# Two-layer hybrid mixer step on one core: value products with 128 weight columns, three more projections by seven products, PSUM copies on ScalarE

## The chip, the cores and the metric

One core of one Trainium2 chip runs the whole program in one launch. The metric is the device time of that launch in microseconds, lower is better; before the change it is 1943.42 us (median of three runs, 1942.09 to 1944.15).

## The reference

Two layers run over 512 prompt positions and 32 sample positions (544 columns in all), model width 1024, in float32. A layer multiplies the residual stream `h` by one wide input projection, whose columns feed four token mixers of four heads of 64 each, and gates:

```
pr = split_projection(h @ w_in)
A: stick-breaking:  z = q k^T / 8; w = exp(log_sigmoid(z) + sum of later log_sigmoid(-z)); y = w v
B: retention:       q, k = rotary(q), rotary(k) / 8; S' = g^c S + (k * decay)^T v
                    o = ((q k^T) * decay) v + (q S) * g^(n+1); y = head_norm(o) * silu(gate)
C: forgetting:      softmax(q k^T / 8 + cq - ck) v
D: sparse:          softmax over the 128 (sample: 72) keys that an indexer picks, one shared k and v head
merged = sum_i sigmoid(gate_i) * (y_i @ w_branch_i)
h = LN(ALPHA h + merged @ w_out); h = LN(ALPHA h + SwiGLU(h))
```

The prompt starts with an empty past, the sample has a cache of 256 positions and a retention state. The outputs are `h` and the new caches and states.

## The kernel before

**Layout.** Activations are kept transposed, features on the partitions and the 544 columns in two halves of `HB` = 272. Each operand of a large product is split into two reduced-precision parts, high (by ScalarE) and low (by VectorE, the remainder), and a product is three TensorE instructions: high x high, high x low, low x high.

**Two kinds of projection.** `dense` (L733) multiplies 128 output columns: weights `raw` are split into `whi` and `wlo`, and for each half eight blocks of depth take three matmuls each, 48 in all, 96 for a pair of column blocks. `strassen` (L786) makes a pair of column blocks for both halves at once with seven products instead of eight (84 matmuls): it needs sums of weight blocks (`ws`, `wt` by accumulating DMAs of GpSimd's queue, `wsum` by VectorE), splits seven operands `wop`, and adds up the results `st`, `su`, `sv` on VectorE. Its right side are differences of `h` blocks, `T`. `proj2` (L921) uses it for retention's values, `merge` (L1653) for all gates, `ffn` for most of the feed-forward part. Retention's queries, keys and gate use `proj` and `dense`.

**Mixers.** `fox` (L1297) and `dsa` (L1373) go through four row blocks and four heads: scores into PSUM, maximum, exponential, division by the sum, four or fewer transposes, a copy `pT` of those out of PSUM, and then the product with the values. That product takes the head's 64 value columns as weights and writes half of the partitions of a bank, `o[r, ...]`, for s = 0 the lower and for s = 1 the upper half. `stick` (L1425) does all heads' products of a row block together; `pv_sample` (L1360) does them for the sample. The values are plain float32, for which one matmul of the program is two passes in the trace.

**Retention** (L1532): the projections of queries and keys are rotated by `rotary` (L1499): four DMAs swap partition groups into `xs`, GpSimd multiplies by the cosine, VectorE by the sine, VectorE adds. Four chunks of 128 columns follow, each with scores, state and `head_norm_T`; the gate's sigmoid is made from exp (ScalarE), add (GpSimd) and reciprocal (VectorE) in `silu` (L1544).

**Copies.** `ev` (L683) copies out of PSUM, on VectorE and ScalarE in turn.

**Order.** Every operation is recorded first (so every instruction of the profile has the line L661, and groups are told apart by tile names). `schedule` (L555) then simulates a list scheduler with its own costs and priorities and sets each engine's order; `fillers` (L637) puts small idle matmuls where that simulation leaves TensorE without work; `places` and `fit` (L180, L206) choose buffer addresses. `build` repeats this up to five times, each from the draft before, and keeps the one whose simulated end is earliest. Each engine's queue runs strictly in the order set.

```
def ev(...):            # L683
    if eng is None:
        self.flip ^= 1
        eng = "v" if self.flip else "s"
...
nc.tensor.matmul(o[r, p * 128:(p + 1) * 128], v[:, j, h * 64:(h + 1) * 64], pT[:, j, :],   # fox
                 start=j == 0, stop=j == i)
```

## Time and profile before

| | us |
|---|---|
| runs before: median (lowest to highest) | 1943.42 (1942.09 to 1944.15) |
| the profiled execution | 1947.43 |
| its span, first to last instruction | 1945.7 |
| TensorE busy in it | 1881.4 (97%) |
| VectorE busy | 1601.7 (82%) |
| ScalarE busy | 1043.9 (54%) |
| GpSimd busy | 499.8 (26%) |

The mean granted TensorE clock over the span is 0.991 of full speed. TensorE's rows are matmuls (PE) and weight loads (PEld), which overlap; a matmul's recorded length is longer than the distance to the next one, so what one costs is read from the distance of starts. The first layer ends at about 970 us, the second begins there.

### The profile page before, as it was taken

What the parts mean: (1) busy time and instruction counts of PE and PEld (TensorE: products, weight loads), DVE (VectorE), ACT (ScalarE), POOL (GpSimd) and SP (SyncE); (2) the same over time, 40 slices, a digit from 0 to 9 for tenths busy, and PEclk for the clock granted to TensorE, in tenths of its full rate; (3) what the DMA queues carried; (4) which work ended last, traced back from release to release, by engine and by line L of the source; (5) the groups of instructions that cost most, each with busy time, mean ns of one, the idle gap of its engine ahead of it and who ended that gap; (6) DMA issues with size and microseconds to landing.
All of it is one profiled execution on the core that took longest, in us unless ns stands there. A gap on an engine that the chain in (4) does not pass through costs nothing.

```text
span 1945.7 us, 39164 instructions
## 1 busy us (share of the span) xinstructions
PE 1881.4 (97%) x14619; PEld 1801.8 (93%) x14619; DVE 1601.7 (82%) x3549; ACT 1043.9 (54%) x2160; POOL 499.8 (26%) x500
## 2 busy tenths in 40 slices
PE   9999999999999999999999999899999999999997
PEld 8997789999998999999989978889999999999996
DVE  5988769787879889888778886697879799899875
ACT  4565535555546656556455563355556375565552
POOL 0343031234341111321413331302433301114101
PEclk9999999999999999999999999999999999999999
DMA  8322244666632687777313132347675237777741
GB/s 226 85 72 69 52 101 91 150 153 144 155 105 77 143 199 168 175 169 182 103 32 99 56 96 52 79 96 162 138 162 154 81 90 171 191 174 175 172 114 47
DMA packets 386879, 241.25 MB, mean 124 GB/s; under 512 B 26728, under 2 KB 363032, under 8 KB 386432
## 3 DMA queue, kind: packets, MB, share of 16 engines
q1 hardware_dynamic: 361344, 193.64, 36.2%
q0 software_dynamic: 25344, 45.10, 13.7%
q8 instruction: 115, 1.88, 0.4%
q14 instruction: 76, 0.62, 0.1%
HBM read 183.55 MB, written 7.82 MB: 98 GB/s over the span
## 4 chain that ended last, share of the span: by engine, by line
PE 35%; DVE 7%; DMA 3%; ACT 2%; issue 2%; POOL 1%; SPq 0%; POOLq 0%; ACTq 0%; DVEq 0%
PE bank L661 35%; DMA ws<-wa 1%; DVE wop L661 1%; DVE lnw L661 1%; DVE wlo L661 1%; DVE y L661 1%; DMA raw<-in_w_ffn_out_dram 0%; DVE st L661 0%; DVE wsum L661 0%; DVE score L661 0%; DVE q L661 0%; DMA xs<-rk 0%; DVE sv L661 0%; ACT whi L661 0%; POOL lnw L661 0%
## 5 line engine op out<-in xcount | busy, mean ns | idle before, releaser
L661 PE MATMUL bank<-T,wop 128*128 128x272 f32 x3456 | 461.3, 289 | 5.5 <-DVE su L661 4.3
L661 PEld LDWEIGHTS bank<-T,wop 128*128 128x128 f32 x3456 | 444.5, 189 | 7.4 <-DVE su L661 5.1
L661 PE MATMUL bank<-h0hi,wop 128*128 128x272 f32 x1152 | 243.9, 291 | 0.5 <-DVE acc L661 0.4
L661 PEld LDWEIGHTS bank<-h0hi,wop 128*128 128x128 f32 x1152 | 189.7, 188 | 3.5 <-DVE acc L661 0.6
L661 POOL DMA_DIRECT2D ws<-wa x88 | 76.9, 874 | 377.1 <-DVE wop L661 133.6
L661 ACT ACTIVATE wop<-raw 128x512 fp32r<-128x512 f32 (+1 forms) x176 | 109.1, 620 | 112.5 <-PE bank L661 101.6
L661 PE MATMUL bank<-h0lo,wop 128*128 128x272 f32 x576 | 165.7, 288 | 0.0
L661 POOL DMA_DIRECT2D wt<-raw x88 | 77.5, 880 | 334.3 <-DVE su L661 47.5
L661 PE MATMUL bank<-q,wop 128*128 128x272 f32 x1176 | 153.7, 290 | 5.9 <-DVE su L661 2.9
L661 PEld LDWEIGHTS bank<-q,wop 128*128 128x128 f32 x1176 | 148.9, 188 | 9.5 <-DVE su L661 3.9
L661 DVE TENSOR_TENSOR wop<-raw,wop 128x512 fp32r<-128x512 f32 (+1 forms) x176 | 125.3, 714 | 31.6 <-ACT wop L661 31.0
L661 PE MATMUL bank<-h0hi,whi 128*128 128x272 f32 (+1 forms) x480 | 147.7, 308 | 3.3 <-ACT h0hi L661 3.3
L661 ACT ACTIVATE wop<-wsum 128x512 fp32r<-128x512 f32 (+1 forms) x176 | 109.0, 620 | 71.7 <-PE bank L661 45.1
L661 DVE TENSOR_TENSOR wlo<-raw,whi 128x1024 fp32r<-128x1024 f32 (+1 forms) x92 | 122.9, 1344 | 29.4 <-PE bank L661 13.4
L661 PE MATMUL bank<-h1hi,whi 128*128 128x272 f32 x480 | 143.8, 300 | 1.2 <-DVE su L661 0.7
L661 PE MATMUL bank<-h0lo,whi 128*128 128x272 f32 (+1 forms) x480 | 140.9, 294 | 1.8 <-DVE h0lo L661 1.8
L661 DVE TENSOR_TENSOR wop<-wsum,wop 128x512 fp32r<-128x512 f32 (+1 forms) x176 | 125.0, 710 | 20.8 <-ACT wop L661 19.7
L661 PE MATMUL bank<-h0hi,wlo 128*128 128x272 f32 (+1 forms) x480 | 141.0, 294 | 1.2 <-DVE wlo L661 1.1
L661 PE MATMUL bank<-h1lo,whi 128*128 128x272 f32 x480 | 139.3, 290 | 0.1
L661 PE MATMUL bank<-h1hi,wlo 128*128 128x272 f32 x480 | 139.3, 290 | 0.0
L661 ACT ACTIVATE whi<-raw 128x1024 fp32r<-128x1024 f32 (+1 forms) x92 | 95.7, 1048 | 81.1 <-PE bank L661 42.0
L661 PE MATMUL bank<-h1hi,wop 128*128 128x272 f32 x576 | 122.6, 291 | 0.7 <-DVE wop L661 0.7
(463 smaller groups left out, 5032.8 us busy)
## 6 DMA issues: line engine op xcount, KB each, us to landing
raw<-in_w_in_dram SPq DMA_DIRECT2D x46, 512.0 KB, 3.7
ws<-wa POOLq DMA_DIRECT2D x80, 256.0 KB, 4.4
wt<-raw POOLq DMA_DIRECT2D x80, 256.0 KB, 4.1
raw<-in_w_ffn_in_dram SPq DMA_DIRECT2D x76, 256.0 KB, 3.8
raw<-in_w_in_dram SPq DMA_DIRECT2D x68, 256.0 KB, 3.4
wa<-in_w_ffn_in_dram SPq DMA_DIRECT2D x38, 256.0 KB, 3.0
ws<-in_w_ffn_in_dram SPq DMA_DIRECT2D x38, 256.0 KB, 3.1
wt<-in_w_ffn_in_dram SPq DMA_DIRECT2D x38, 256.0 KB, 4.0
```

What stands on the lines that cost most here:

```text
L661: call(*a, **k)
```

## The change

1. **Products with values** take 128 weight columns: the value columns of both heads of a pair. All partitions of the bank are written for each head, and only the right half is read, by the new `ev_heads` (two copies of 64 partitions instead of one of 128). DSA's shared value head is doubled side by side (`vv`, and its cache twice).
2. **Retention's queries, keys and gate** use `proj2`; the factor 0.125 of the keys moves into constants.
3. **The sigmoid** is exp(-ln(1 + exp(-x))), three ScalarE instructions.
4. **`ev`** uses ScalarE alone.
5. `SPLITS[3]`: the low parts in `proj2` that GpSimd made are made by VectorE.
6. The planner tries four settings of (spare, margin) from one first draft, instead of a chain of five drafts.

```diff
-SPLITS = ("vvvvvvv", "vvvvvvv", "vvvvvvv", "vgvgvgv")
+SPLITS = ("vvvvvvv", "vvvvvvv", "vvvvvvv", "vvvvvvv")
-SPARE = 10.0
-MARGIN = 5.0
-TRIES = 5
+FITS = ((10.0, 5.0), (5.0, 5.0), (10.0, 2.0), (10.0, 10.0))
...
     def ev(self, out, in_, scale=None, eng=None):
         nc = self.nc
         if eng is None:
-            self.flip ^= 1
-            eng = "v" if self.flip else "s"
+            eng = "s"
...
-    def proj2(self, col, names):
+    def proj2(self, col, names, use=None):
+        if use:
+            r = self.blocks(*(self.i["w_in"][self.l][:, col + c * 128:col + c * 128 + 128] for c in range(2)), 4)
+            for j, x in enumerate(self.strassen(r, 4, self.xt, None, SPLITS[3], "d")):
+                use(j // 2, j % 2, x)
+            return
         out = self.fm(names)
...
-                        nc.tensor.matmul(o[r, p * 128:(p + 1) * 128], v[:, j, h * 64:(h + 1) * 64], pT[:, j, :],
+                        nc.tensor.matmul(o[:, h * 128:(h + 1) * 128], v[:, j, p * 128:(p + 1) * 128], pT[:, j, :],
                                          start=j == 0, stop=j == i)
-            self.ev(y[:, :, i * 128:(i + 1) * 128], o[:, :256].rearrange("a (p q) -> a p q", p=2))
+            self.ev_heads(y, o, i * 128, 128)
...
-                    nc.tensor.matmul(o[s * 64:(s + 1) * 64, p * 32:(p + 1) * 32], v(kr, j, h),
-                                     pT[:kr, j, h * 32:(h + 1) * 32], start=j == 0, stop=j == 2)
-        self.ev(y[:, :, T:NT], o[:, :64].rearrange("a (p q) -> a p q", p=2))
+                    nc.tensor.matmul(o[:, h * 32:(h + 1) * 32], v(kr, j, p), pT[:kr, j, h * 32:(h + 1) * 32], start=j == 0,
+                                     stop=j == 2)
+        self.ev_heads(y, o, T, 32)
+
+    def ev_heads(self, y, o, c0, n):
+        for s in range(2):
+            r = slice(s * 64, s * 64 + 64)
+            self.ev(y[r, :, c0:c0 + n], o[r, :4 * n].rearrange("a (p s q) -> a p s q", p=2, s=2)[:, :, s])
...
+        vv = self.mem.tile([128, 4, 128], F32, name="vv")
+        for s in range(2):
+            self.ev(vv[:, :, s * 64:s * 64 + 64], tmk[:, :, 64:128], eng="s")
...
-                        nc.tensor.matmul(o[r, p * 128:(p + 1) * 128], tmk[:, j, 64:128], pT[:, j, :],
-                                         start=j == 0, stop=j == i)
+                        nc.tensor.matmul(o[:, h * 128:(h + 1) * 128], vv[:, j, :], pT[:, j, :], start=j == 0, stop=j == i)
...
-                        nc.tensor.matmul(o[s * 64:(s + 1) * 64, p * 128:(p + 1) * 128], v[:, j, h * 64:(h + 1) * 64],
+                        nc.tensor.matmul(o[:, h * 128:(h + 1) * 128], v[:, j, p * 128:(p + 1) * 128],
                                          w[:, a + p * 128:a + (p + 1) * 128], start=j == 0, stop=j == i)
...
-        q = self.rotary(self.proj(COL["ret_q"], "rq0"), cs)
-        k = self.rotary(self.proj(COL["ret_k"], "rk0", 0.125), cs)
+        q = self.rotary(self.proj2(COL["ret_q"], "rq0"), cs)
+        k = self.rotary(self.proj2(COL["ret_k"], "rk0"), cs)
...
             nc.scalar.activation(se[:, c, cs], ps, AF.Exp, scale=-1.0)
-            nc.gpsimd.tensor_scalar(se[:, c, cs], se[:, c, cs], 1.0, None, op0=OP.add)
-            nc.vector.reciprocal(se[:, c, cs], se[:, c, cs])
+            nc.scalar.activation(se[:, c, cs], se[:, c, cs], AF.Ln, bias=1.0)
+            nc.scalar.activation(se[:, c, cs], se[:, c, cs], AF.Exp, scale=-1.0)
             nc.vector.tensor_tensor(sg[:, c, cs], se[:, c, cs], ps, op=OP.mult)
-        for c in range(2):
-            a = COL["ret_g"] + c * 128
-            raw = self.load([(self.i["w_in"][l][:, a:a + 128], 0, 128)], 8)
-            self.dense(raw, 0, 128, 8, self.hx,
-                       lambda h, ps: silu(c, h, ps))
+        self.proj2(COL["ret_g"], "rg", silu)
```

What it moves in the engines' orders, at three places.

**TensorE, DSA in the second layer**, third row block (`pT` is the transposed probability, `tmk` or `vv` the values, `du` the next head's probabilities to be transposed; a row names the bank written, the moving operand and the weights, and the partitions and columns written). Before:

```order
L661 MATMUL bank_67<-pT_1844,tmk_1547 64x128 x3
L661 MATMUL bank_66<-ident_70,du_1845 128x128 x3
L661 MATMUL bank_62<-h0hi_1510,whi_1883 128x272
L661 MATMUL bank_62<-h0lo_1511,whi_1883 128x272
L661 MATMUL bank_62<-h0hi_1510,wlo_1884 128x272
L661 MATMUL bank_60<-h1hi_1512,whi_1883 128x272
```

and after:

```order
L660 MATMUL bank_67<-pT_1873,vv_1828 128x128 x3
L660 MATMUL bank_66<-ident_70,du_1874 128x128 x3
L660 MATMUL bank_60<-h0hi_1538,wop_1932 128x272
L660 MATMUL bank_60<-h0lo_1539,wop_1932 128x272
L660 MATMUL bank_60<-h0hi_1538,wop_1932 128x272 x2
L660 MATMUL bank_60<-h0lo_1539,wop_1932 128x272
```

The products write 128 partitions, and the work that stands between a head's products and the next one's comes from a seven-product projection.

**TensorE, the end of retention in the first layer** (`oc` is the normed output, `rk` the keys, `kd` the decayed keys, `rvt` the values; `yhi`, `ylo` and `wb` belong to the merge). Before:

```order
L661 MATMUL bank_66<-ident_70,oc_508 128x128 x2
L661 MATMUL bank_63<-yhi_529,wb_536 128x272
L661 MATMUL bank_63<-ylo_530,wb_536 128x272
L661 MATMUL bank_63<-yhi_529,wb_536 128x272
L661 MATMUL bank_60<-yhi_529,wb_536 128x272
L661 MATMUL bank_60<-ylo_530,wb_536 128x272
...
L661 MATMUL bank_66<-ident_70,rk_568_451 128x128 x2
L661 MATMUL bank_60<-yhi_529,wb_536 128x272
...
L661 MATMUL bank_66<-rvt_475,kd_510 128x128 x2
```

and after:

```order
L660 MATMUL bank_66<-ident_70,oc_536 128x128 x2
L660 MATMUL bank_66<-ident_70,rk_578_461 128x128 x2
L658 MATMUL bank_60<-idle_72 128x128
...
L660 MATMUL bank_66<-rvt_494,kd_538 128x128 x2
...
L660 MATMUL bank_66<-ident_70,oc_544 128x128 x2
...
L660 MATMUL bank_66<-ident_70,rk_578_461 32x128 x2
...
L660 MATMUL bank_66<-rvts_495,kd_548 128x128 x2
...
L660 MATMUL bank_66<-ident_70,oc_554 128x32 x2
```

Where merge matmuls stood between the last steps of retention, idle matmuls stand alone (9, 12, 9, 9, 3 and 5 of them, each left-out stretch holding nothing else).

**VectorE, the rotation of the keys in the second layer** (`xs` the swapped keys, `wop` operands of the seven products, `su` and `st` their sums, which free PSUM banks). Before:

```order
L661 TENSOR_TENSOR xs_1888<-xs_1888,cs_1872 128x1088
L661 TENSOR_TENSOR wop_1904<-wsum_1897,wop_1904 128x512
L661 TENSOR_TENSOR rk_2463_1881<-rk_2463_1881,xs_1888 128x1088
L661 TENSOR_TENSOR su_1895<-st_1894,bank_60 128x272
L661 TENSOR_TENSOR wlo_1911<-raw_1909,whi_1910 128x1024
```

and after:

```order
L660 TENSOR_TENSOR xs_1935<-xs_1935,cs_1901 128x1088
L660 TENSOR_TENSOR wop_1964<-raw_1956,wop_1964 128x512
L660 TENSOR_TENSOR wop_1965<-ws_1958,wop_1965 128x512
L660 TENSOR_TENSOR rk_2501_1919<-rk_2501_1919,xs_1935 128x1088
L660 TENSOR_TENSOR su_1942<-st_1941,bank_62 128x272
```

The rotation's addition stands ahead of the same `su` in both; two operands stand ahead of it instead of one, and what follows is the next seven products instead of a dense block.

## Rows read from the trace of the kernel before

**Rows 1.** The page's first part: busy time, share of the span and instructions of each engine.

```profile
PE 1881.4 (97%) x14619; PEld 1801.8 (93%) x14619; DVE 1601.7 (82%) x3549; ACT 1043.9 (54%) x2160; POOL 499.8 (26%) x500
```

**Rows 2.** Who TensorE waited for: us in total, times, longest us.

```profile
PE bank L661 <- DVE su L661: 8.4, 8, 3.5
PE bank L661 <- DVE sg L661: 1.2, 1, 1.2
```

**Rows 3.** Stretches of the span: start and end, length, then busy us (and instructions) of PE, PEld, DVE, ACT and POOL, granted clock, DMA share, GB/s. Fox of the first layer, retention of the first and of the second layer, merge of the first layer.

```profile
165.00:213.00 48.00, 44.42 (x346) 36.95 (x344) 41.31 (x147) 22.96 (x66) 6.38 (x6) 0.99 0.28 73
269.00:334.00 65.00, 62.29 (x478) 57.69 (x476) 56.69 (x141) 27.43 (x52) 13.76 (x14) 1.00 0.41 97
1231.00:1302.00 71.00, 64.98 (x476) 60.24 (x477) 57.05 (x140) 29.07 (x54) 14.60 (x16) 0.95 0.38 89
310.00:480.00 170.00, 167.95 (x1314) 164.24 (x1315) 138.93 (x286) 95.01 (x183) 46.49 (x51) 1.00 0.62 143
```

**Rows 4.** TensorE in order of time, a stretch of seven products in the second layer: start us, length us, what, how many.

```profile
1231.60 4.71 PE L661 MATMUL bank<-T,wop 128*128 128x272 f32 x36
1236.14 0.29 PE L661 MATMUL bank<-h0hi,wop 128*128 128x272 f32 x1
```

**Rows 5.** The same view in DSA of the second layer, products with 64 value columns ("128*64") between dense matmuls and transposes.

```profile
1198.19 0.29 PE L661 MATMUL bank<-h1hi,wlo 128*128 128x272 f32 x1
1198.41 0.65 PE L661 MATMUL bank<-pT,tmk 128*64 128x128 f32 x4
1199.00 0.44 PE L661 MATMUL bank<-ident,du 128*128 128x128 f32 x2
...
1216.45 1.09 PE L661 MATMUL bank<-pT,tmk 128*64 128x128 f32 x8
1217.46 0.65 PE L661 MATMUL bank<-ident,du 128*128 128x128 f32 x4
```

**Rows 6.** The same view in retention of the second layer, float32 products with 128 weight columns.

```profile
1285.96 0.56 PE L661 MATMUL bank<-rvt,A 128*128 128x64 f32 x4
1286.35 0.44 PE L661 MATMUL bank<-S,qd 128*128 128x128 f32 x2
...
1288.38 0.44 PE L661 MATMUL bank<-ident,rk 128*128 128x128 f32 x2 [0.51 <-DVE y_ret L661]
...
1289.60 0.29 PE L661 MATMUL bank<-yhi,wb 128*128 128x272 f32 x1
1289.72 0.61 PE L661 MATMUL bank<-rvt,kd 128*128 128x128 f32 x4
...
1290.29 0.29 PE L661 MATMUL bank<-ylo,wb 128*128 128x272 f32 x1
```

**Rows 7.** Groups of equal matmuls over the whole span, by shape: busy us, mean ns of one | idle before them and what ended it.

```profile
L661 PE MATMUL bank<-pT,fvt 128*64 128x128 f32 x160 | 24.3, 282 | 4.8 <-DVE pT L661 2.5 <-ACT pT L661 1.2 <-DVE sm L661 0.9
L661 PE MATMUL bank<-sw,svt 128*64 128x128 f32 x160 | 16.5, 281 | 0.3 <-ACT sw L661 0.3
```

**Rows 8.** TensorE in order of time, the sample's products of stick-breaking and of DSA in the second layer, and what follows each.

```profile
1133.83 1.03 PE L661 MATMUL bank<-sws,vccache_sb_v 128*64 128x32 f32 x24
1134.79 0.66 PE L661 MATMUL bank<-ident,fv 128*128 128x128 f32 x4
...
1228.82 2.37 PE L661 MATMUL bank<-pT,vccache_dsa_v 128*64 128x32 f32 x24
1231.12 0.39 PE L661 MATMUL bank<-h0hi,wop 128*128 128x272 f32 x1
```

**Rows 9.** The gate's sigmoid, over the span: ns of one (least, median, most), first and last start, shape.

```profile
L661 POOL TENSOR_SCALAR se<-se x8: 891/892/1187, 287.7 to 1261.1; 128x272 f32<-128x272 f32 x8
L661 DVE RECIPROCAL se<-se x8: 1839/1852/1854, 288.6 to 1262.0; 128x272 f32<-128x272 f32 x8
```

**Rows 10.** The rotation of the keys in the second layer: VectorE, then GpSimd, then TensorE in order of time, then ten us around it as a stretch (columns as in Rows 3).

```profile
1234.40 1.29 DVE L661 TENSOR_TENSOR xs<-xs,cs 128x1088 f32<-128x1088 f32 x1 [2.95 <-DMA xs<-rk]
1235.61 3.02 DVE L661 TENSOR_TENSOR wop<-wsum,wop 128x512 fp32r<-128x512 f32 x1
1238.56 2.35 DVE L661 TENSOR_TENSOR rk<-rk,xs 128x1088 f32<-128x1088 f32 x1
...
1234.50 3.59 POOL L661 TENSOR_TENSOR rk<-rk,cs 128x1088 f32<-128x1088 f32 x1 [5.05 <-DMA xs<-rk]
...
1241.31 3.09 PE L661 MATMUL bank<-T,wop 128*128 128x272 f32 x12 [3.49 <-DVE su L661]
...
1237.00:1247.00 10.00, 6.51 (x33) 6.29 (x31) 6.96 (x6) 1.34 (x2) 4.43 (x4) 0.68 0.49 109
```

**Rows 11.** Groups of equal instructions on VectorE and ScalarE over the span, by shape (columns as in Rows 7).

```profile
L661 DVE TENSOR_TENSOR wlo<-raw,whi 128x1024 fp32r<-128x1024 f32 x90 | 121.5, 1357 | 29.4 <-PE bank L661 13.4 <-ACT whi L661 9.5 <-issue 2.5
L661 DVE TENSOR_TENSOR wop<-raw,wop 128x512 fp32r<-128x512 f32 x160 | 116.5, 730 | 31.6 <-ACT wop L661 31.0
...
L661 ACT ACTIVATE wop<-raw 128x512 fp32r<-128x512 f32 x160 | 100.7, 630 | 105.6 <-PE bank L661 95.0 <-DMA wt<-in_w_ffn_in_dram 2.8 <-ACT g L661 2.6
L661 ACT ACTIVATE whi<-raw 128x1024 fp32r<-128x1024 f32 x90 | 94.3, 1056 | 78.4 <-PE bank L661 42.0 <-DMA raw<-in_w_out_dram 16.0 <-DMA raw<-in_w_ffn_out_dram 7.5
```

**Rows 12.** Weight loads, by shape (columns as in Rows 7): 64 float32 columns, 128 float32 columns.

```profile
L661 PEld LDWEIGHTS bank<-pT,tmk 128*64 128x64 f32 x160 | 16.6, 136 | 5.9 <-issue 1.5 <-DVE mx L661 0.6 <-ACT pT L661 0.6
L661 PEld LDWEIGHTS bank<-rvt,kd 128*128 128x128 f32 x32 | 4.2, 190 | 0.5
```

More of the change, by code (lines that the diff above doesn't have):

```diff
@@ L153, with __init__ @@
     GRAIN = 64
-    def __init__(self, plan, whole, banks, before=None, virtual=None):
+    def __init__(self, plan, whole, banks, before=None, virtual=None, fit=()):
         self.plan, self.whole, self.banks, self.before = plan, whole, banks, before
@@ L161, in __init__ @@
         self.users, self.blockers = {}, {}
-        self.at = before.places(virtual) if self.stage > 1 else None
+        self.at = before.places(virtual, *fit) if self.stage > 1 else None
     def buffer(self, size, lead=0):
@@ L178, in bank, with places @@
         return View(self.banks[k][:], b)
-    def places(self, virtual):
+    def places(self, virtual, spare, margin):
         if self.stage == 1:
@@ L193, in places @@
                 ready[i] = min((ops[j].start for j in true[i].then), default=op.start) - (op.done - op.start) - 1.0
-            ready[i] = max(ready[i], min(op.latest, op.start) - MARGIN)
+            ready[i] = max(ready[i], min(op.latest, op.start) - margin)
         start, end = np.full(n, 1e9), np.full(n, -1e9)
@@ L200, in places @@
             try:
-                return self.fit(start, end, cells, long)
+                return self.fit(start, end, cells, long, spare)
             except MemoryError as e:
@@ L204, in places, with fit @@
         raise error
-    def fit(self, start, end, cells, long):
+    def fit(self, start, end, cells, long, spare):
         size, born, last = (np.array(x) for x in (self.size, self.born, self.last))
@@ L217, in fit @@
             over = np.where(early, end - start[b], np.where(late, end[b] - start, 1e9))
-            cost = np.full(cells, -SPARE)
-            for x in np.flatnonzero(done & (over > -SPARE)):
+            cost = np.full(cells, -spare)
+            for x in np.flatnonzero(done & (over > -spare)):
                 c = cost[at[x]:at[x] + size[x]]
@@ L1026, in cache_k, with cache_v @@
         return kc
-    def cache_v(self, name, w):
-        vc = self.mem.tile([128, 3, w], F32, name="vc" + name)
+    def cache_v(self, name, w, times=1):
+        vc = self.mem.tile([128, 3, w * times], F32, name="vc" + name)
         src = self.i[name][self.l, 0]
@@ L1032, in cache_v @@
             src = src.rearrange("n h d -> n (h d)")
-        self.nc.sync.dma_start(vc[:, 0:2, :], src.rearrange("(t p) c -> p t c", p=128))
+        for j in range(times):
+            self.nc.sync.dma_start(vc[:, 0:2, j * w:(j + 1) * w], src.rearrange("(t p) c -> p t c", p=128))
         self.nc.gpsimd.memset(vc[:, 2, :], 0.0)
@@ L1407, in dsa @@
         pT = self.softmax_T(z, NKS, mx[:, 1:2], False)
-        self.pv_sample(pT, lambda kr, j, h: vc[:kr, j, :], y)
+        self.pv_sample(pT, lambda kr, j, p: vc[:kr, j, :], y)
         return y
@@ L2012, in build, with collect @@
         scratch = [dr.tile([4, T], F32, name=f"scratch{n}") for n in range(DEPTH)]
-        def collect(nc, memory, before, virtual=None):
+        def collect(nc, memory, before, virtual=None, fit=FITS[0]):
             plan = Plan(nc)
-            mem = plan.mem = Memory(plan, memory, banks, before, virtual)
+            mem = plan.mem = Memory(plan, memory, banks, before, virtual, fit)
             plan.place("SB", whole, SBUF)
@@ L2029, in build @@
         count = draft(None)
-        virtual = mem = draft(count)
+        virtual = draft(count)
+        first = draft(virtual, virtual)
         best = None
-        for _ in range(TRIES):
-            before = mem
+        for fit in FITS:
             try:
-                mem = draft(mem, virtual)
+                end = draft(first, virtual, fit).plan.end
             except MemoryError:
-                break
-            if best is None or mem.plan.end < best[0]:
-                best = mem.plan.end, before
-        final = collect(tc.nc, whole, best[1], virtual)
+                continue
+            if best is None or end < best[0]:
+                best = end, fit
+        final = collect(tc.nc, whole, first, virtual, best[1])
         with tc.manual_schedule():
```

20 lines of the change are left out of this document (11 added, 9 removed).

## The prediction

> **What bounds the kernel now.** I read the busy times first [rows 1]: TensorE is busy 97% of the span, VectorE 82%, ScalarE 54%. TensorE's list of waits [rows 2] is short; its largest single wait is 3.5 us, for VectorE's `su`. The stretches [rows 3] say the same stage by stage: in the merge TensorE is idle 2 of 170 us, in fox 3.6 of 48, in the second layer's retention 6.0 of 71, there at a mean granted clock of 0.95. So TensorE's stream is the bound, and a matmul removed from it is worth its full step; VectorE follows at 80 to 87% of those stretches, near enough to become the wait wherever its load bunches up. What a matmul costs is the distance between starts, not the recorded length.
>
> **The seven-product projections.** In a run of seven products 36 matmuls lie between 1231.60 and 1236.14 us, 0.126 us each [rows 4]. A dense pair of column blocks takes 96, the seven products 84; six projections change (three in each layer): 6 x 12 = 72 matmuls fewer, 72 x 0.126 = **-9.1 us**, all on the bound.
>
> What it puts on VectorE per projection: two `wlo` at 1.36 us go, seven `wop` at about 0.73 come [rows 11], with two weight sums of about the same size and half a dozen additions of results; about +5 us for 10.6 us of TensorE work. The whole change takes off VectorE eight reciprocals of 1.85 us [rows 9] and every PSUM copy, so that the sum of its work falls by some 25 us (an estimate from these rows) and that of ScalarE rises by some 80: 58% instead of 54%. I cost both at nothing on average. ScalarE has the room: it is busy 23 of 48 us in fox [rows 3]. VectorE does this very mixture at 82% in the merge while TensorE stays at 99% [rows 3]. If that cover goes, `su` and `st` come late, and with them the PSUM banks of the next seven products. The queues: each projection issues five quarter-megabyte loads on SP for two of half a megabyte, and two accumulating DMAs on GpSimd's queue; one of those now stands behind the 3.59 us rotation multiply [rows 10]. The loads run blocks ahead, so I price that at nothing, and with the rotation's rival below if it comes late.
>
> **The value products of fox and DSA.** A product with 64 value columns enters late and leaves late. The last dense matmul before one starts at 1198.19, the product at 1198.41 [rows 5]: 0.22 instead of 0.126, so 0.09 to get in. Four passes then take 0.59 until the transposes start, eight take 1.01 [rows 5]; that is 0.17 + 0.105 per pass. Each mixer and layer has four heads with 2, 4, 6 and 8 passes, 64 groups in all: 16 x (0.38 + 0.59 + 0.80 + 1.01) = 44.5 us, and 64 x 0.09 = 5.8 to get in. With 128 columns the nearest rows are retention's state products, same type and same 128 moving columns: from 1289.60 to 1290.29 lie four passes and two ordinary matmuls, (0.69 - 0.25) / 4 = 0.110 each, with no extra on either side [rows 6]. 320 passes at 0.110 are 35.2. Gain 44.5 + 5.8 - 35.2 = 15.1. In fox some products wait for `pT` or the sum anyway (4.8 us of idle time [rows 7]), and there the entry is not on the path: I take off 1.1. **-14.0 us**; bounds -9.3 (no entry gained) and -15.1.
>
> The columns themselves speak against the change, and this is where the trace and the notes part. The trace: a load of 64 float32 columns is recorded at 136 ns, one of 128 at 190 [rows 12], yet the pass with 128 columns steps at 0.110 [rows 6], no more than the 0.105 of one with 64. The Trainium skill (TensorE: Matmul & The Clock Gate, LDWEIGHTS) makes the load's time proportional to its columns whatever their depth, an estimate of 53 ns for 64 and 107 for 128; by that rule, were the load not covered, these 320 passes would cost about 17 us more and the term would turn to +3. By the row it is covered, and I go by the row.
>
> **The value products of stick and of the sample.** Stick has 160 passes in 16 runs, 16.5 us busy [rows 7], which is about 15.4 in steps (a run's last recorded length reaches 0.07 into the next instruction). With 64 columns, neighbours on different halves of the array overlap; at 0.110 each, the passes come to 17.6, less 16 entries of 0.09: **+0.8**. The sample's runs of 24 take 0.96 (stick) and 2.30 us (DSA; fox alike) [rows 8], 2 x 0.96 + 4 x 2.30 = 11.1 in both layers. With 128 columns and few moving ones the nearest row is `rvt,A`, four passes in 0.39 [rows 6]: 144 x 0.098 = 14.1, less six entries: **+2.5** (bounds 0 and +5).
>
> **Waits that go or come.** The gate's bank was held through GpSimd's add and the reciprocal; TensorE waited 1.2 us for `sg` once [rows 2]: **-1.2**. In the first layer the last six steps of retention lose their cover, the merge matmuls (the second place shown in the order). A bare step of that kind, from the keys' transpose at 1288.38 to the product with them at 1289.72, lasts 1.34 us even with other work between [rows 6]; six are 8.0. Zero is the other end, if the chip's VectorE gets there sooner than the planner thought. I take half: **+4**. The rotation's stall in the second layer (3.49 us, and a clock of 0.68 over ten us, which is another 3.2 lost at the lower level of 1.2 instead of 2.4 GHz [rows 10]) stays as it is: GpSimd's multiply still slows a 0.73 us operand to 3.02, and `su` still stands behind the addition (the third place). Bounds for this and its three sisters: -6.7 if it goes, +13.4 if two more become like it.
>
> **Sum:** -9.1 - 14.0 + 0.8 + 2.5 - 1.2 + 4 = -17.0. The profiled execution took 1947.4, 4.0 above the median of the runs; against it 1930.4, against the median 1943.4 it is **1926.4 us**.
>
> **The rivals.** *Waits leave as well.* VectorE and GpSimd lose work around retention; the bare steps cost nothing and the rotation's stall with its clock goes: -4 - 6.7, **1915.7**. For it: the low parts of `proj2` leave GpSimd, which shares its hold on VectorE. Against it: the multiply itself is unchanged.
>
> *The rotation stalls more often.* Queries and keys of both layers are now rotated in the middle of seven products, whose operands come from the engine that the multiply holds up. Two more stalls like the one seen, 2 x 6.7: **1939.8**. For it: 3.02 us for one operand [rows 10]. Against it: the queries' rotation in the second layer caused no such wait although it holds VectorE alike, and much prepared work lies ahead.
>
> *ScalarE's copies lengthen fox.* All copies of `pT` go through one queue, where weight parts have priority. If each of the 16 copies of fox that move waits for one `whi` of 1.06 us [rows 11], that is +17: **1943**. The Trainium skill (TensorEngine Tiling (Array Packing), PSUM Bottleneck) advises using both engines for emptying PSUM; the trace has ScalarE less than half busy in fox [rows 3].
>
> *The weight loads are not hidden (slower).* All 624 passes with values load 54 ns more [rows 12]; if each pays it, +33.7: **1960**. It decides from 27 ns per pass, where the other terms are used up. The state products speak against it, but they come in fours, not in eights between softmax steps.
>
> That the change does not do what it says is no rival: the built order has the 128-row products and 72 matmuls fewer.
>
> **Chances.** Forecast 0.63 (own range 1918 to 1934), waits leave 0.13, rotation 0.14, ScalarE 0.05, weight loads 0.05. What a measurement can tell here is about 0.2%, 3.9 us. The forecast, the first rival and nearly half of the second lie below 1939.5: faster 0.82; the rest of the second and the third within: same 0.12; slower 0.06. The range leaves out the two last rivals, half of the rotation's and the best of the first: 1912 to 1940.
>
> **What would show it.** In the profile after: 504 more matmuls of `wop` and 576 fewer of `whi` and `wlo`; products with values entered at 0.126 after a dense matmul and followed at 0.11 per pass; their recorded loads at 190 ns and no idle time before them; VectorE below 1601 us, ScalarE near 1125. Wrong would be: passes at 0.15 or more, TensorE waiting for `pT` from ScalarE by more than 5 us in all, or a clock at the lower level in retention more than once a layer.

## The result, and the profile after

The changed kernel takes **1955.32 us** (median of four runs, 1954.66 to 1958.57) against 1943.79 for the kernel before, measured beside it: ratio 1.0054, interval 1.0031 to 1.0077. It is 11.5 us slower. The forecast was 1926.4 in a range from 1912 to 1940; the result lies outside, on the other side of no change.

The page's first part after answers to [rows 1]. VectorE lost 28 us and ScalarE gained 72, where the forecast had some 25 and some 80. TensorE is busy 4.5 us longer with 72 real matmuls fewer (504 more of `wop`, 576 fewer of `whi` and `wlo`, as forecast).

```profile
PE 1885.9 (96%) x14600; PEld 1822.7 (93%) x14600; DVE 1574.1 (80%) x3494; ACT 1116.3 (57%) x2369; POOL 500.0 (26%) x498
```

TensorE in order of time, the fourth row block of DSA in the second layer after, the place of [rows 5]: eight passes with 128 columns are entered 0.12 us after the start of the last projection matmul and take 0.89, 0.111 each. The forecast had 0.126 and 0.110.

```profile
1229.36 0.29 PE L660 MATMUL bank<-h0hi,wop 128*128 128x272 f32 x1
1229.48 1.05 PE L660 MATMUL bank<-pT,vv 128*128 128x128 f32 x8
1230.37 0.38 PE L660 MATMUL bank<-ident,ck 128*64 128x128 f32 x2
```

The same view after at the sample's products, the kind of [rows 8], with what follows each run: fox in the first layer, then stick-breaking, fox and DSA in the second. They take 3.47, 2.60, 4.13 and 6.04 us; before it was 0.96 for stick-breaking and 2.30 for the others. The first two ran at the full clock, the last two wholly or in part at the lower one.

```profile
224.88 3.54 PE L660 MATMUL bank<-pT,vccache_fox_v 128*128 128x32 f32 x24
228.35 0.47 PE L660 MATMUL bank<-ident,du 128*128 128x128 f32 x1
...
1142.71 2.76 PE L660 MATMUL bank<-sws,vccache_sb_v 128*128 128x32 f32 x24
1145.31 0.63 PE L660 MATMUL bank<-ident,fv 128*128 128x128 f32 x4
...
1191.68 4.20 PE L660 MATMUL bank<-pT,vccache_fox_v 128*128 128x32 f32 x24
1195.81 0.47 PE L660 MATMUL bank<-ident,du 128*128 128x128 f32 x1
...
1240.79 6.12 PE L660 MATMUL bank<-pT,vccache_dsa_v 128*128 128x32 f32 x24
1246.83 0.59 PE L660 MATMUL bank<-h0hi,wop 128*128 128x272 f32 x1
```

Stretches after, columns as in [rows 3]: the bare end of retention in the first layer, the layer boundary, and DSA's sample in the second layer. In each the granted clock falls to its lower level for a part of the time, and in the last stretch it is 0.52, so nearly all of 14 us runs at 1.2 GHz.

```profile
317.00:334.00 17.00, 12.74 (x97) 11.00 (x96) 9.83 (x33) 3.27 (x10) 1.17 (x2) 0.80 0.20 40
...
970.00:1000.00 30.00, 20.51 (x157) 19.09 (x155) 22.62 (x54) 16.56 (x38) 6.35 (x2) 0.89 0.20 54
...
1238.00:1252.00 14.00, 13.65 (x59) 13.15 (x60) 7.93 (x9) 2.63 (x8) 4.42 (x2) 0.52 0.20 39
```

**Where the time went.** I split the distance from each matmul's start to the next in the trace. First comes a yardstick step for its shape at the higher clock (moving columns / 2.4 GHz + 0.0125 us, at least 0.109, fitted to the trace: 0.126 for 272 columns as in [rows 4]). Then comes what the lower clock adds to that. The rest are waits and small delays, with those at the value products apart; passes shorter than the yardstick, as the sample's at 64 columns, come out negative. Idle matmuls stand in waits, and the time from their starts is counted with the waits. In us, of one profiled execution each; the last four columns are versions from the experiments. The last row says how far that execution lay from its version's median, so differences of a few us between columns are not safe.

| | before | after | e3 | e9 | e5 | e14 |
|---|---|---|---|---|---|---|
| real matmuls, yardstick steps | 1793.5 | 1784.4 | 1784.4 | 1784.4 | 1784.4 | 1784.4 |
| fox, DSA passes beyond | 16.7 | 8.3 | 7.1 | 7.4 | 7.4 | 7.4 |
| stick-breaking beyond | -0.1 | 1.9 | 0.8 | 0.0 | -0.6 | 0.9 |
| sample beyond | -3.9 | 3.5 | 4.3 | -3.7 | -3.5 | -3.5 |
| lower clock | 10.2 | 18.7 | 16.3 | 18.1 | 4.8 | 8.5 |
| other waits with the idle matmuls in them, small delays | 115.1 | 124.9 | 113.2 | 125.7 | 120.6 | 117.9 |
| sum | 1931.5 | 1941.7 | 1926.0 | 1931.9 | 1913.0 | 1915.6 |
| the execution's time less the median | +3.6 | +3.3 | -0.5 | +3.7 | -2.2 | +1.0 |

From before to after: -9.1 for the projections and -8.4 in fox and DSA, as meant; +2.0 and +7.4 in stick-breaking and the sample, +8.5 lower clock, +9.8 other waits with their idle matmuls.

### The profile page after: what moved, and what is told of

The parts are those of the page before. It is cut to its first block, busy times and chain, and to the rows that moved or that the text cites. A ratio compares the mean times of both kernels' runs of the same rounds, so it can differ in the third digit from the quotient of the medians.

```text
span 1956.8 us, 39346 instructions
## 1 busy us (share of the span) xinstructions
PE 1885.9 (96%) x14600; PEld 1822.7 (93%) x14600; DVE 1574.1 (80%) x3494; ACT 1116.3 (57%) x2369; POOL 500.0 (26%) x498
## 4 chain that ended last, share of the span: by engine, by line
PE 70%; DVE 13%; DMA 7%; ACT 5%; issue 3%; POOL 1%; SPq 1%; POOLq 0%; ACTq 0%; DVEq 0%
PE bank L660 69%; DMA ws<-wa 3%; DVE wop L660 3%; DVE lnw L660 2%; DVE wsum L660 1%; DVE st L660 1%; POOL lnw L660 1%; DMA raw<-in_w_ffn_in_dram 1%; DVE y L660 1%; DVE q L660 1%; SPq L660 1%; DMA ws<-in_w_ffn_in_dram 1%; DMA ws<-in_w_in_dram 1%; ACT wop L660 0%; DVE sv L660 0%
## 5 line engine op out<-in xcount | busy, mean ns | idle before, releaser
L660 PE MATMUL bank<-T,wop 128*128 128x272 f32 x3744 | 510.5, 290 | 2.7 <-DVE su L660 2.1
L660 PEld LDWEIGHTS bank<-T,wop 128*128 128x128 f32 x3744 | 485.1, 189 | 6.6 <-DVE su L660 3.8
L660 PE MATMUL bank<-h0hi,wop 128*128 128x272 f32 x1248 | 271.0, 295 | 1.6 <-DVE su L660 1.0
L660 PEld LDWEIGHTS bank<-h0hi,wop 128*128 128x128 f32 x1248 | 209.5, 191 | 5.9 <-DVE su L660 1.4
L660 DVE TENSOR_TENSOR wlo<-raw,whi 128x1024 fp32r<-128x1024 f32 (+1 forms) x80 | 104.1, 1307 | 32.9 <-ACT whi L660 13.4
L660 PEld LDWEIGHTS bank<-h0lo,wop 128*128 128x128 f32 x624 | 119.4, 191 | 0.0
L660 PE MATMUL bank<-h0hi,whi 128*128 128x272 f32 (+1 forms) x384 | 116.0, 302 | 3.1 <-ACT h0hi L660 3.1
L660 PE MATMUL bank<-h0lo,whi 128*128 128x272 f32 (+1 forms) x384 | 112.2, 292 | 2.4 <-DVE h0lo L660 2.0
L660 PE MATMUL bank<-h1hi,whi 128*128 128x272 f32 (+1 forms) x384 | 113.0, 294 | 0.1
L660 PE MATMUL bank<-h1lo,whi 128*128 128x272 f32 (+1 forms) x384 | 111.2, 290 | 1.0 <-DVE h1lo L660 1.0
L660 PE MATMUL bank<-h0hi,wlo 128*128 128x272 f32 (+1 forms) x384 | 111.3, 290 | 0.0
```

What stands on the lines that cost most here:

```text
L660: call(*a, **k)
```

## The experiments

Two theories stood first. **A**: the sample's passes are the mis-sized term. **P**: the new search of the planner picks an order with more waits. Rivals: copies on ScalarE (S), VectorE or other chains setting the pace (V). Where only the shape of the value products changes, the planner's costs do not, so every engine keeps its order; e1, e2, e5, e6, e9 and e14 use that. "Chain" is the kernel before's search.

**e4, how far two runs of one program differ.** The kernel before with the new search.

```diff
-        for _ in range(TRIES): ...            # chain of drafts
+        for fit in FITS: ...                  # four settings, one first draft
```

> The kernel before with the new search alone (four settings from one first draft). Theory P: slower than the kernel before by 5 to 15 us, 1949 to 1959, with more waits at the layer boundary or in the sample stretches. Rival S: no change, 1940 to 1947.

1945.26 us, ratio 1.0017 (1.0003 to 1.0030). The built order turned out to be that of the kernel before, instruction by instruction. So this says nothing of the search, but it shows that a difference of 2 us here means nothing. The kernel before, measured again beside each set of versions, had medians from 1941.34 to 1943.81; comparisons between sets carry that too.

**e1, e2: value products back to 64 columns, order of the changed kernel.**

```diff
-  nc.tensor.matmul(o[:, h * 32:(h + 1) * 32], v(kr, j, p), pT[:kr, ...], ...)
+  nc.tensor.matmul(o[s * 64:s * 64 + 64, h * 32:(h + 1) * 32], v(kr, j, p)[:, s * 64:s * 64 + 64], pT[:kr, ...], ...)
```

> The changed kernel with the sample's value products alone back at 64 weight columns; order of every engine unchanged, only these 144 passes differ. Theory A (the forecast mis-sized them: in the trace after the six sample runs take 11 us more than before, where the forecast had 2.5): the six runs return to 11 us in all and the time falls by 7 to 9 us, to about 1947. Theory B (the low clock right behind these runs, 6.8 us in fox and 13.7 us in DSA of the second layer, is also their doing, since the array does little in passes of 32 columns): a further 5 to 8 us go, to about 1940. Rival C (they only fill time in which TensorE would wait for the softmax of the sample anyway): no change, 1955.

> The changed kernel with all value products (fox, DSA, stick-breaking, sample) back at 64 weight columns, each writing its own half of the partitions, every engine's order unchanged. By the steps in the trace after, 128 columns gain 8 us in fox and DSA where the forecast had 14, lose 2 in stick-breaking and 7 in the sample: nothing is left. Theory A: 1952 to 1957, the same as the changed kernel. Rival (the forecast's sizes hold, -14.0 + 0.8 + 2.5): about 10.7 us slower than the changed kernel, 1966.

e1: 1948.94, 6.4 less than the changed kernel. e2: 1950.03, 5.3 less, a little below Theory A's range. Theory B's further 5 to 8 us did not come. The sample's columns cost time, and in this order the change loses by having all four kinds at 128; the rival of 1966 falls. The six runs of e1 spread from 1940.67 to 1952.57, all below the changed kernel's lowest of 1954.66: the sign is safe, the size to a few us.

**e3: the changed kernel with the chain search.**

```diff
-        for fit in FITS:
-            end = draft(first, virtual, fit).plan.end ...
+        for _ in range(5):
+            before = mem; mem = draft(mem, virtual) ...
```

> The changed kernel with the planner's search of before (a chain of five drafts) in place of the four settings from one first draft. Theory P (the waits, idle matmuls and low clock that the trace after has beyond before, some 20 us, come with the order that the new search picks): the time falls by 8 to 20 us, 1935 to 1947. Rival S (they come from work that moved: copies on ScalarE alone, operands of the seven products on VectorE): 1952 to 1960 whichever search is used.

1943.35, ratio 0.9999 (0.9984 to 1.0014): 12.0 less with the same work. The chain's order is the one that the new search gets from its first setting, (10, 5); it chose the second, (5, 5), whose simulated end is 0.3 us earlier (1870.0 against 1870.2). What the planner held for a small gain was 12 us slower on the chip. In the table e3 has 11.7 us less of other waits and 2.4 less lower clock.

**e5, e6, e14: value products in the chain's order.** e5: stick-breaking and sample at 64; e6: all at 64; e14: only the sample at 64 (edits as in e1).

> The chain-search version of the changed kernel with the value products of stick-breaking and of the sample at 64 weight columns, fox and DSA at 128, every engine's order as in that version. Theory A (the 128-column passes of these two lose 8 us, 6 of them in the sample): 8 us less than the chain-search version, about 1935, and 8 less than the kernel before. Rival C (the sample's loss shows only in the order of the changed kernel, behind its wait for the DSA sample's softmax): 1940 to 1944.

> The same with fox and DSA at 64 columns as well. Theory G (their steps shrink by 8 to 10 us, but the next wait that another engine's chain ends gives most of it back: the sample's softmax behind a late weight sum, the layer boundary behind GpSimd's lnw): 2 to 4 us slower than with fox and DSA at 128, about 1938. The forecast (14 us gained, on the bound): 14 slower, about 1949.

> The chain-search version with only the sample at 64 weight columns, stick-breaking at 128. Theory A (of the 11.2 us for both, the sample has the most: 7 us of steps and the low clock behind them): 1933 to 1936. Rival (stick-breaking's 160 passes have half of it): 1937 to 1940.

e5: 1932.13, 11.2 below e3. e14: 1931.5, ratio 0.9942 (0.9926 to 0.9958): **the sample alone costs 11.8**, stick-breaking nothing that can be told. e6: 1943.66, so fox and DSA at 128 columns gain 11.5; their passes lose 9.8 (17.2 to 7.4 beyond the yardstick step). Theory G falls in this order. e6 and e3 take the same time (1943.66 and 1943.35): what fox and DSA gain by 128 columns, the sample loses. The sample in the second layer's fox, TensorE in order of time, first e3, then e14:

```profile
1188.10 4.32 PE L660 MATMUL bank<-pT,vccache_fox_v 128*128 128x32 f32 x24 [0.42 <-ACT pT L660]
1192.36 0.47 PE L660 MATMUL bank<-ident,du 128*128 128x128 f32 x1
```

```profile
1178.75 2.37 PE L660 MATMUL bank<-pT,vccache_fox_v 128*64 128x32 f32 x24 [0.43 <-ACT pT L660]
1181.06 0.33 PE L660 MATMUL bank<-ident,du 128*128 128x128 f32 x1
```

The wait is the same and the order is the same; 24 passes take 4.26 us instead of 2.31. Part of the 4.26 is at the lower clock; in the first layer, at the full clock, it is 3.48 for 2.30. And the clock falls during these runs or within 2 us behind them, in e3 at four of the six, in e14 at one. Here are e3's two in the second layer, stick-breaking's sample and fox's (stretches, columns as in [rows 3]):

```profile
1136.00:1143.00 7.00, 7.00 (x51) 6.87 (x49) 3.31 (x9) 4.57 (x11) 6.09 (x5) 0.76 0.12 42
1188.00:1198.00 10.00, 9.89 (x49) 9.21 (x50) 4.63 (x23) 3.72 (x16) 0.00 (x0) 0.66 0.14 33
```

The same two places in e14, where the second still has one short dip:

```profile
1128.00:1135.00 7.00, 5.78 (x63) 5.14 (x62) 4.90 (x17) 5.97 (x16) 6.32 (x5) 1.00 0.20 71
1178.00:1188.00 10.00, 9.23 (x65) 8.37 (x64) 6.29 (x28) 5.80 (x22) 0.00 (x0) 0.83 0.14 33
```

**e9: e5's work in the changed kernel's order.**

> The changed kernel in its own order, value products of stick-breaking and of the sample at 64 weight columns, fox and DSA at 128: the same work as the version of 1932 us, and only the order of the planner's search differs. Theory P (the new search's order costs some 12 us, bare retention in the first layer and VectorE's softmax steps behind a late weight sum): 1943 to 1948. Rival (with the sample's low clock gone the two orders are worth the same): 1930 to 1936.

1945.04, 10.3 below the changed kernel and 12.9 above e5: theory P. The same comparison of the two orders can be made at two more shapes of the value products: with all at 64 columns the changed kernel's order costs 6.4 (e6 to e2), with the sample alone at 64 it costs 17.4 (e14 to e1). So the order costs something every time, from 6 to 17 us, and is not one number.

Where is it lost? In the profiled executions of these four pairs (e3 and the changed kernel, e5 and e9, e6 and e2, e14 and e1) the last merge matmul of the first layer starts 2.6 us earlier, 2.2 later, 2.6 earlier and 1.2 later in the changed kernel's order. That of the second layer starts 12.3, 16.1, 8.6 and 13.0 later. So the loss lies between the two merges, at the layer boundary and in the second layer, and not at the bare end of retention in the first.

In the table 13.3 of the 18.9 us between the profiled executions of e9 and e5 is lower clock; the medians are 12.9 apart. Stretches of e9, then the same places of e5: the end of retention and the boundary in the first layer, the second layer's DSA sample, its end of retention.

```profile
317.00:334.00 17.00, 13.66 (x103) 12.37 (x104) 8.26 (x21) 2.13 (x6) 0.85 (x1) 0.80 0.26 56
970.00:1000.00 30.00, 23.96 (x154) 22.94 (x155) 22.24 (x54) 16.20 (x39) 6.34 (x2) 0.77 0.17 49
1225.00:1245.00 20.00, 17.47 (x107) 15.91 (x107) 11.85 (x17) 7.39 (x20) 4.72 (x4) 0.74 0.43 98
1278.00:1292.00 14.00, 12.32 (x78) 11.03 (x77) 11.45 (x39) 8.28 (x14) 0.00 (x0) 0.76 0.19 45
```

```profile
320.00:334.00 14.00, 12.54 (x91) 10.45 (x91) 12.62 (x39) 7.10 (x16) 0.85 (x1) 1.00 0.33 75
970.00:1000.00 30.00, 26.17 (x204) 25.32 (x203) 21.86 (x55) 19.49 (x49) 3.31 (x6) 0.94 0.01 4
1210.00:1230.00 20.00, 19.02 (x154) 17.53 (x152) 12.85 (x24) 10.80 (x26) 7.34 (x9) 1.00 0.56 119
1262.00:1276.00 14.00, 13.72 (x107) 12.16 (x106) 13.71 (x47) 8.61 (x18) 0.00 (x0) 1.00 0.18 44
```

**e13, e16: more idle matmuls**, in the changed kernel and in e5, nothing else moved.

```diff
-    WARM = 0.55, 3.41
+    WARM = 0.8, 3.41
```

> The changed kernel with more idle matmuls where its plan leaves TensorE idle (the filler's share 0.8 for 0.55), every other instruction in its place. In the trace of the changed kernel 14 us of TensorE's time goes to doubled steps at half clock in nine stretches before the tail, after waits. Theory K (the order costs by the low clock behind its waits, and idle matmuls in the planned ones prevent it): 5 to 10 us faster than the changed kernel, 1945 to 1950. Rival (the waits that are not in the plan cause it, or the idle matmuls themselves delay real ones): 1953 to 1962.

> The version of 1932 us with more idle matmuls (share 0.8). Theory K: little low clock is left in it (5 us of doubled steps, the tail's among them), so 0 to 3 us faster, 1929 to 1932. Rival (idle matmuls delay real ones): 1933 to 1938.

e13: 1965.07, a median slower by 9.8, above the rival's range too; two of its six runs took 1954.50, the changed kernel's time, and the other four 1964.47 to 1967.43. e16: 1932.85, no change. The profiled execution of e13 is one of the two quick ones: in it the lower clock costs 9.5 instead of 18.7, and the time from idle matmuls' starts is 39.0 instead of 29.5 (525 of them instead of 255). What the slower four lose is not seen in it. Filling is no remedy here: none of the six is clearly faster, so theory K's 5 to 10 us did not come. How much of the order's cost the clock causes by itself stays open.

**e11: fox and DSA alone at 128 columns in the kernel before.** The edits are those of the change's `fox` and `dsa`, `ev_heads` and `vv`, and nothing else of it.

> The kernel before with the value products of fox and DSA alone at 128 weight columns (copies in turn on both engines, dense projections, search as before). The forecast: 14 us faster than before, 1929. By the step between the two chain-search versions, 10 to 11.5: 1932. Theory G (given back where another engine's chain ends the next wait): 1939 to 1944.

1934.4, ratio 0.9953 (0.9935 to 0.9970): 9.4 faster, in an order of its own; between the forecast and Theory G, near the estimate from e5 and e6.

**e7, e10, e17, e18: the projections.** e7 and e10 are e3 and e5 with dense queries, keys and gate. e17 adds to e5 an idle matmul ahead of each three matmuls of the six projections; e18 as many to six products of seven in the merges.

```diff
-        q = self.rotary(self.proj2(COL["ret_q"], "rq0"), cs)      # keys alike; gate by dense(...)
+        q = self.rotary(self.proj(COL["ret_q"], "rq0"), cs)       # e7, e10
...
+            for j in range(self.ops[i].extra if ...):             # e17, e18: 168 in all
+                self.real.tensor.matmul(out, x, x, start=False, stop=True, ...)   # x: the idle tile
```

> The chain-search version of the changed kernel with retention's queries, keys and gate as dense products again (96 matmuls for a pair of column blocks, in place of 84), all else as changed. The forecast (72 matmuls at 0.126 us on the bound, VectorE's additions hidden): 9 us slower than the chain-search version, about 1952. Theory V (in the mixers VectorE's and GpSimd's chains set the pace, so that fewer matmuls only mean longer waits, and the accumulating transfers that the seven products need come late): no slower, 1938 to 1945.

> The chain-search version with stick-breaking and sample at 64 columns (1932 us), and retention's queries, keys and gate dense again. The forecast (72 matmuls at 0.126 us on the bound): 9 us slower, 1941. Theory V (in the mixers the chains of the other engines set the pace, so the matmuls saved come back as idle time, in the first layer above all): no slower than 1936.

> The version of 1932 us with 168 idle matmuls (28 in each of the six projections of queries, keys and gate, one ahead of each three matmuls), every other instruction in its place. In the planned gaps one of them steps at 0.056 us, so this is some 9.3 us of TensorE work put back where the seven products saved 9.1. The forecast (the projections' matmuls lie on the bound): 8 to 10 us slower, 1940 to 1942. Theory V (they fill time in which other chains set the pace): 0 to 4 us slower, 1932 to 1936.

> The control: the same 168 idle matmuls in six products of seven of the two merges, where TensorE is busy 99% of the time. Every theory: 9 us slower, 1940 to 1942; it says what such a matmul costs where nothing hides it.

e7: 1943.15 against 1943.35; e10: 1932.27 against 1932.13. Dense projections cost nothing that can be told, twice. But e17 takes 1953.58, 21.4 more than e5, and the control e18 1957.54, 25.4 more; their runs overlap (1948.58 to 1959.52 and 1950.82 to 1959.69), so work put into the projections costs about what it costs in the merge. Both miss their numbers, since an idle matmul put between others costs more than 0.056. In the merge it steps at 0.039 and the next matmul at 0.21 instead of 0.126, which is 0.125 for each and 21 us for 168; the rest is lower clock and waits. TensorE in order of time, e18 in the first layer's merge:

```profile
389.00 0.23 PE L661 MATMUL bank<-idle 128*128 128x128 bf16 x1
389.04 0.37 PE L663 MATMUL bank<-h0hi,wop 128*128 128x272 f32 x1
389.25 0.28 PE L663 MATMUL bank<-h0lo,wop 128*128 128x272 f32 x1
389.37 0.29 PE L663 MATMUL bank<-h0hi,wop 128*128 128x272 f32 x1
389.50 0.23 PE L661 MATMUL bank<-idle 128*128 128x128 bf16 x1
```

This speaks against theory V's reason, that the projections fill time in which others set the pace: time added there shows nearly in full. It does not show what time taken away there gains, for where a second chain is nearly as long, adding costs and removing gains nothing. The 9.1 us are given back somewhere: from e10 to e5 the split shows -9.1 of real matmuls and -2.6 of lower clock, and +9.6 of waits with the idle matmuls and the passes of fox and DSA. Of TensorE's waits over 0.15 us, those for ScalarE come to 20.8 us in e5 and 16.6 in e10, to 18.8 in e3 and 13.4 in e7. Two of them, e5, then e10 (us in total, times, longest):

```profile
PE bank L660 <- ACT pT L660: 7.7, 12, 1.5
...
PE bank L660 <- ACT tmm L660: 3.7, 2, 3.2
```

```profile
PE bank L660 <- ACT pT L660: 3.2, 5, 1.4
...
PE bank L660 <- ACT tmm L660: 1.1, 2, 0.7
```

So longer waits for ScalarE take the place of a part of the matmuls, while those for VectorE's `su` fall (3.7 in e5, 8.3 in e10). Since the two versions differ in order as well, whether the seven operands on ScalarE or the order does it is not settled.

**e8, e12, e15: the copies.** e12 puts all on ScalarE in the kernel before; e8 and e15 put e3's and e5's back in turn.

```diff
         if eng is None:
-            eng = "s"
+            self.flip ^= 1                       # e8, e15; e12 is the reverse
+            eng = "v" if self.flip else "s"
```

> The chain-search version of the changed kernel with the copies out of PSUM on VectorE and ScalarE in turn again. The forecast (copies cost nothing where they are): no change, 1941 to 1946. Theory S (ScalarE's queue, in which weight parts run, holds back the transposed probabilities and the keys): 4 to 10 us faster, 1933 to 1939. Theory V (VectorE is what the mixers wait for, so its load counts): 3 to 6 slower, 1946 to 1949.

> The kernel before with all copies out of PSUM on ScalarE alone. The forecast (they cost nothing where they are): 1941 to 1946. Theory V (VectorE sets the pace of the mixers, so 25 us less on it shortens waits): 3 to 8 us faster, 1935 to 1940. Theory S (ScalarE's queue delays the transposed probabilities): 4 to 15 slower, 1947 to 1958.

> The version of 1932 us (chain search, stick-breaking and sample at 64 columns) with the copies out of PSUM on both engines in turn. Copies on ScalarE alone cost 10 us in the kernel before, and copies in turn 21 us in the chain-search version. Theory O (neither engine's copies as such, but the order that the planner makes for them; the largest waits move with it): anything from 1925 to 1955, with the difference in a few single waits and the low clock. Theory V (copies in turn cost VectorE what it lacks): 1950 to 1955, with many small waits for VectorE.

e12: 1954.04, 10.2 slower. e8: 1964.4, 21 slower than e3 and outside all three numbers; e15: 1952.76, 20.6 slower than e5, in the range of O and of V. Copies on ScalarE cost in one program and gain in the other, so neither engine's copies are dear as such; each edit makes the planner order everything anew. Theory V's many small waits for VectorE are not there: TensorE waits 35.0 us for it in e15 (49 times) and 31.2 in e5 (44 times). This leaves theory O, argued from the signs and not shown at a fixed order. The sigmoid and the moved low parts were not tried alone. The parts of the change do not add up across orders, and single edits are told apart only to some 10 us unless the order is held.

## Why the prediction was wrong, step by step

The forecast missed by three steps: the sample's passes were sized from a row with other moving columns, the matmuls saved in the projections were credited in full, and the new search was priced by one place that is not where it loses.

- **Projections, -9.1: the step in TensorE's stream right, the credit wrong.** The yardstick steps fell by exactly 9.1 and added work there shows (e17, e18), but undoing the saving costs nothing (e7, e10). The step that failed is that a matmul removed from TensorE's stream "is worth its full step"; the text also costed the operands and accumulating transfers "at nothing". Longer waits took the place of the matmuls; which chain ends them is open.
- **Fox and DSA, -14.0: mechanism right, size high.** Entry and step came as read: before, the passes take 44.2 us where the forecast had 44.5. With 128 columns, all at the full clock in e5, they take 38.0 where it had 35.2: in 23 of the 64 groups the first pass takes about 0.21 us and not 0.11, nearly always where TensorE enters the group late. Measured: -9.4 (e11), -11.5 (e6 to e5), -5.0 in the changed kernel's order (e2 to e9, with runs of e9 from 1938.78 to 1959.93). They lie on both sides of the lower bound, -9.3.
- **Stick-breaking, +0.8:** nothing that can be told (e5, e14).
- **Sample, +2.5 with bounds 0 and +5: the term that failed.** It measured 11.8 in one order and 6.4 in the other. The row taken, `rvt,A` [rows 6], has 64 moving columns. With 32 the load is no longer covered: 24 passes of fox in the first layer take 0.145 us each (3.47 / 24) at full clock, against 0.096 [rows 8], and stick-breaking's 0.108 (2.60 / 24) against 0.040. The differences, 49 and 68 ns, lie about the 54 ns by which a load of 128 columns is longer than one of 64 [rows 12]; the loads of such a run start 0.11 us apart (median), and with 64 columns 0.056 in fox's. The Trainium skill (TensorE: Matmul & The Clock Gate, LDWEIGHTS) makes a load's time proportional to its columns, an estimate of 53 ns for the 64 added; these passes agree with it. The rival "weight loads are not hidden" was right for these passes and wrong for most of the 480 others; I gave it one price for all. By the table the steps are 7.8 us of the cost (e3 to e14) and the lower clock during and behind the passes another 7.8, with 4.7 more of other waits against them; the term did not have the clock.
- **The planner's search, not a term: 12 us** (e3; 6.4 to 17.4 over the four pairs). I listed it as a part of the change and priced only one consequence, the bare end of retention in the first layer, +4 with bounds 0 and 8. That place is not where the order loses. The first layer's merge, which holds these steps, takes 226.3 us for 218.1, but it begins 6.1 earlier than before, and its last matmul starts 2.6 us earlier than in e3. The same kind of bare place at the boundary and at DSA's sample I did not look for. At DSA's sample the trace after shows the chain: GpSimd's accumulation of a weight sum, issued at 1230.71, lands at 1236.09; VectorE's sum, which reads its result, starts at 1236.16 after 2.13 us of waiting, and the softmax of DSA's sample stands behind it in the queue. TensorE then waits 2.22 for `pr`, and the stretch at 0.52 follows. The sum is of a gate in the merge, made by seven products in both kernels, so it is no work of the added projections; what costs is its place ahead of the softmax. VectorE, GpSimd, TensorE of the changed kernel in order of time:

```profile
1233.58 0.45 DVE L660 TENSOR_REDUCE mx<-bank 128x1 f32<-128x288 f32 x1
1236.16 0.69 DVE L660 TENSOR_TENSOR wsum<-ws,raw 128x512 f32<-128x512 f32 x1 [2.13 <-issue]
1236.77 0.15 DVE L660 TENSOR_SCALAR mx<-mx 128x1 f32<-128x1 f32 x1
...
1230.71 0.87 POOL L660 DMA_DIRECT2D ws<-wa  x1 [2.43 <-DMA ws<-in_w_in_dram]
...
1238.35 0.60 PE L660 MATMUL bank<-ident,pr 128*128 128x128 f32 x3 [2.22 <-DVE pr L660]
```

In e3's order no weight sum stands between the two steps of the softmax, and TensorE waits 0.54, for another engine. In the changed kernel's order the wait for `pr` is 2.53 in e9, 4.59 in e1 and none in e2, the pair with the smallest price; in e5, e6 and e14, which have e3's, it is at most 0.54. VectorE, then TensorE of e3:

```profile
1228.96 0.45 DVE L660 TENSOR_REDUCE mx<-bank 128x1 f32<-128x288 f32 x1
1229.44 0.15 DVE L660 TENSOR_SCALAR mx<-mx 128x1 f32<-128x1 f32 x1
...
1231.86 0.52 PE L660 MATMUL bank<-ident,pr 128*128 128x128 f32 x3 [0.54 <-ACT st L660]
```

- **Copies, at nothing:** TensorE waits 3.2 us for `pT` from ScalarE in the changed kernel, below the 5 that I named, so the fox rival (+17) did not happen; in e5's order it is 7.7.
- **The keys' rotation:** the wait of 3.49 for `su` [rows 10] is gone although a 0.73 us operand still takes 2.99; the wait for `pr` took its place just ahead.
- **Signs named:** passes at 0.11 and loads at 190 came true for fox, DSA and stick-breaking. Two signs of being wrong came too: passes at 0.15 or more (the sample's in the second layer, 4.13 / 24 and 6.04 / 24), and a clock that fell more than once in the second layer's retention.

The forecast beside what was measured along one path, from the kernel before (1943.1 in that set) over e6, e5 and e3 to the changed kernel, by medians. Along a path the parts add up by construction; along another they are other numbers, as said above.

| | forecast | measured | miss |
|---|---|---|---|
| projections, `sg` and everything else (before to e6) | -10.3 | +0.5 | +10.8 |
| fox and DSA (e6 to e5) | -14.0 | -11.5 | +2.5 |
| stick-breaking and sample (e5 to e3) | +3.3 | +11.2 | +7.9 |
| the search; forecast: bare steps (e3 to after) | +4.0 | +12.0 | +8.0 |
| sum | -17.0 | +12.2 | +29.2 |

## What to carry to other kernels

Price a widened weight load by the moving columns of each use: what a pass of 128 mostly hid here, a pass of 32 paid, and in e3 the clock fell at four of six runs of such passes. Where a planner orders the program anew, a row-by-row sum holds only for the order in which the rows were read; compare versions at a fixed order, and treat a change of the search as a term of its own, for a gain of 0.3 us in the planner's simulation was a loss of 12 on the chip. The lowest median measured is that of the changed kernel with the earlier search and the sample at 64 columns (e14), 1931.5 us, ahead of both kernels.

## What the runs showed of the hardware that was not expected

- A pass of a float32 product with 128 weight columns steps at 0.111 us with 128 moving columns, and with 32 it is no shorter: 0.108 in stick-breaking's sample and 0.145 in fox's (with 64 weight columns 0.040 and 0.096).
- A group of passes with 128 weight columns that TensorE enters late has a first pass of about 0.21 us instead of 0.11 (in e5 21 of the 25 late groups of fox and DSA, and 2 of the 39 others). Why is open.
- Over the runs of all versions, a mean granted clock lower by 0.001 went with 1.4 us more of the same program (a common slope through each program's runs); the kernel before, at a mean of 0.993, and the changed one, at 0.985, differ by 8 such steps and by 11.5 us. That the two agree proves nothing: e3, at 0.987, takes the time of the kernel before. It is a companion, not a cause shown.
- An idle matmul (bf16) put between others costs 0.125 us in the merge (e18), 0.039 of its own and the rest in the next matmul's step; in a gap one steps at 0.056.
